# Reloading the residual in single steps, and preferring copies out of PSUM over weight casts

## The chip, the cores and the metric

The kernel runs on one core of a Trainium2 chip. The core has a matrix engine (TensorE, PE in the profile; PEld is its loading of the stationary operand), a vector engine (VectorE, DVE), a scalar engine (ScalarE, ACT), a general engine (GpSimd, POOL) and a queue engine (SyncE, SP), each with an instruction queue of its own, and 16 DMA engines between them. Matmuls write to PSUM, from which DVE and ACT copy or compute into SBUF. The metric is the device time of one execution in microseconds, the median of three runs; smaller is better.

## The reference

Two layers of a decoder trunk over 256 tokens of width 2048, all in fp32. Layer 0 mixes two recurrent branches, layer 1 is a matrix memory (mLSTM). What both do around the mixer is what matters here:

```
for i in range(DEPTH):                       # DEPTH = 2
    hn = rmsnorm(h, norm[i])
    y = mixer_i(hn)                          # layer 1: q, k, v, two gates, mLSTM, head norm, gates
    h = h + y @ w_out[i]                     # output projection, residual add
    pl = rmsnorm(p[i] @ ple_w[i], ple_norm[i])        # p[i]: 256 x 256
    h = h + sigmoid(h @ ple_gate_w[i]) * pl  # gated per-layer embedding
return rmsnorm(h, final_norm)
```

## The kernel before

Every fp32 product is made of three matmuls on parts: each operand x is split into hi, x rounded to the matrix engine's fp32r format, and lo = x - hi, and hi*hi, hi*lo and lo*hi are added up. Weights come in as tiles of 128 x 1024 (`raw`, 512 KB, five buffers, loaded by SP). For each, ACT makes `whi` (line 135) and DVE makes `wlo` (line 136), with four buffers of each. The tokens' operand is split in the same way beforehand (`ahl`, lines 149 and 150). A projection is computed in chunks of 512 output columns; a chunk has two halves of 128 tokens and four quarters of the contraction, and one quarter takes two weight tiles and 24 matmuls (`quarter_tok`, lines 185 to 200). There are three PSUM buffers `mm` and three `mx`.

The program is traced from Python in one order and then planned: a planner lists each engine's instructions in the order in which they would be ready by its own reckoning of times, and the lower number wins among those that are ready. An instruction's number is its place in the trace, less an offset where it stands in `tc.high_priority(offset=...)`. The weight casts of lines 135 and 136 have 400. On the chip each engine then takes its instructions strictly in the planned order, and semaphores hold it where data or a buffer is not there yet. `tc.issue_after(x)` puts an instruction behind x on the same engine.

Side work is written as generators in named lanes. `start` adds one, `step` advances a lane to its next `yield`, `drain` runs it to its end, and `pump`, called once in each quarter, advances every lane by one step, behind the latest cast, matmul and hop of each engine (lines 64 to 85). A transposition from tokens to features is such side work: DVE transposes 32 x 32 blocks into `w` (line 613 or 484), POOL issues a DMA to DRAM (line 600) and four more back into `r` (line 603, a hop), and ACT and DVE finish it (line 631, then 149 and 150; in `to_features` lines 500 and 502).

Layer 1 ends like this, in trace order:

- the last gate projection in the loop of lines 1318 to 1331. Its products `A`, `E`, `B` are in the three `mm` buffers, and partial sums `p1`, `p15` and `g` are in two tiles of the pool tag "h"; lines 274 to 280 form the sums, lines 1323 to 1329 apply the gates, and lane `fm0` to `fm3` transposes each result `u` for the output projection;
- the reload of the residual, lines 1332 to 1336: the hidden state h, which was put into DRAM after layer 0 (`away`), comes back in four tiles `hq` of 128 x 2 x 512 (512 KB each) in the tag "h", whose four buffers until then hold the partial sums and the combined operands of the gate projections;
- the embedding product p[1] @ ple_w[1], `embed`, line 1345: four weight tiles, four groups of 12 matmuls (line 438), one per chunk of 512 columns, each with two token halves in two `mm` buffers. The first half is copied into `pl` by ACT (line 450) and the second by DVE (line 448). The copies have no priority in layer 1 (`first` is None) and 600 in layer 0;
- the output projection, `out_proj`, line 1371, with 16 quarters. Its chunks come from `chunks`: the first two are interleaved, so that chunk 0 is complete after the seventh quarter. Each complete chunk is added to `hq` (line 521), then its transposition starts. The lane "emb", started just before, holds the embedding's norm and gains, and loads rows of gains (line 468).

The reload before:

```
hq = []
for c in range(4):
    t = hp.tile([P, 2, 512], F32, name="hq", tag="h")
    gp.dma_start(out=t, in_=away[c])
    hq.append(t)
```

Of the kernel before, what the change touches and what calls it, by code (L numbers as in the profile page):

```python
# [11 lines left out]
F32 = mybir.dt.float32  # L12
# [7 lines left out]
P = 128  # L20
# [23 lines left out]
def trunk(ctx: ExitStack, tc: tile.TileContext, a, out):  # L44
    nc = tc.nc
    v, s, gp, te, sy = nc.vector, nc.scalar, nc.gpsimd, nc.tensor, nc.sync
# [4 lines left out]
    hp = ctx.enter_context(tc.tile_pool(name="hp", bufs=4))  # L51
# [12 lines left out]
    def start(lane, gen):  # L64
        lanes.setdefault(lane, []).append(gen)

    def step(lane):
        q = lanes.get(lane)
        while q:
            if next(q[0], lanes) is not lanes:  # L70
                return True
            q.pop(0)
        return False
# [8 lines left out]
    def drain(*which):  # L82
        for lane in which:
            while step(lane):
                pass
# [38 lines left out]
    def load_weights(src, pieces=(1, 1), halves=(0, 1), rooms=None):  # L124
        parts = []
        for hf in halves:
            raw = wp.tile([P, 1024], F32, name="raw", tag="raw", bufs=5)
            hi, lo = rooms(hf) if rooms else (wp.tile([P, 1024], F32R, name=n, tag=n) for n in ("whi", "wlo"))
            n = 1024 // pieces[hf]
            for c in range(0, 1024, n):  # L130
                r, h, l = (x[:, c:c + n] for x in (raw, hi, lo))
                sy.dma_start(out=r, in_=block(src, hf * 1024 + c, n))
                with ExitStack() as order:
                    order.enter_context(tc.high_priority(offset=400))
                    last["act"] = s.copy(h, r).ins  # L135
                    last["dve"] = v.tensor_tensor(out=l, in0=r, in1=h.bitcast(F32), op=ALU.subtract).ins  # L136
            parts.append((hi, lo))
        return parts
# [19 lines left out]
    def tokens(x, k, hf):  # L158
        return x[:, k, hf * P:(hf + 1) * P]
# [230 lines left out]
    def load_head(src):  # L390
        praw = tp.tile([P, 512], F32, name="praw", tag="hn", bufs=3)
        raw = wp.tile([P, 1024], F32, name="raw", tag="raw", bufs=5)
        hi, lo = (wp.tile([P, 1024], F32R, name=n, tag=n) for n in ("whi", "wlo"))
        ph, pl, both = act_pair()

        def piece(x, n):
            return x[:, n * T:(n + 1) * T]

        for q, dst, of, n in ((sy, praw, a["pT"][0], 0), (s, raw, src, 0), (gp, raw, src, 1), (s, raw, src, 2),
                              (sy, praw, a["pT"][0], 1), (sy, raw, src, 3)):  # L400
            q.dma_start(out=piece(dst, n), in_=block(of, n * T, T))
        with tc.high_priority(offset=900):
            for n in range(4):
                if n < 2:
                    v.tensor_copy(ph[:, n], piece(praw, n))
                    v.tensor_tensor(out=pl[:, n], in0=piece(praw, n), in1=ph[:, n].bitcast(F32), op=ALU.subtract)
                s.copy(piece(hi, n), piece(raw, n))
                v.tensor_tensor(out=piece(lo, n), in0=piece(raw, n), in1=piece(hi, n).bitcast(F32), op=ALU.subtract)
        return (hi, lo), (ph, pl, both)

    def embed(w, pact, tile_of, first=None):

        pls = []
        for b in range(2):
            head = first and b == 0
            if head:
                part, pact = load_head(w[0])
                parts = [part] + load_weights(w[0], (1, 2), (1,))
            else:
                parts = load_weights(w[b], *(((2, 1),) if first else ()))  # L420
            if first and b:
                first()
            for c, (hi, lo) in enumerate(parts):
                terms = [(hf, k, x, y, 0, 512) for hf in range(2) for k in range(2) for x, y in ((0, 0), (0, 1), (1, 0))]
                if head:
                    terms.sort(key=(lambda t: (t[3], t[3] and t[0], t[1])) if c == 0 else
                               (lambda t: (t[1], t[3] if t[1] == 0 else t[0], t[3])))
                    if c == 0:
                        terms[0:4] = [(hf, 0, x, 0, o, T) for o in (0, T) for x in range(2) for hf in range(2)]
                pool, name = (px, "mx") if first and c == 0 else (pm, "mm")  # L430
                ps = [pool.tile([P, 512], F32, name=name, tag=name) for _ in range(2)]
                halves = []
                for n, (hf, k, x, y, o, w_) in enumerate(terms):
                    mine = [m for m, t in enumerate(terms) if t[0] == hf]
                    with ExitStack() as behind:
                        if first and "pe" in last:
                            behind.enter_context(tc.issue_after(last["pe"]))
                        last["pe"] = te.matmul(ps[hf][:, o:o + w_], tokens(pact[x], k, hf),  # L438
                                               (hi, lo)[y][:, k * 512 + o:k * 512 + o + w_],
                                               start=(n == mine[0]), stop=(n == mine[-1])).ins  # L440
                    if n < mine[-1]:
                        continue
                    pl = tile_of()
                    with ExitStack() as order:
                        if first:
                            order.enter_context(tc.high_priority(offset=600))
                        if hf and (b or not first):
                            v.tensor_copy(pl, ps[hf])
                        else:
                            s.copy(pl, ps[hf])  # L450
                    halves.append(pl)
                pls.append(halves)
        return pls
# [61 lines left out]
    def out_proj(hq, parts, lane):  # L515

        act = {}
        for c, ps in enumerate(parts):
            with tc.high_priority(offset=100):
                for hf in range(2):  # L520
                    v.tensor_tensor(out=hq[c][:, hf], in0=ps[hf], in1=hq[c][:, hf], op=ALU.add)
            start(f"{lane}{c}", to_features(hq[c], c, act, None, lane))
            step(f"{lane}{c}")
        return act
# [17 lines left out]
    def small(n, name, rows=P):  # L542
# [6 lines left out]
    m0_scope = ExitStack()  # L549
    m0 = m0_scope.enter_context(tc.tile_pool(name="m0", bufs=2))  # L550
    pls = embed(a["pw"], None, lambda: p0.tile([P, 512], F32, name="pl", tag="pl"),
                lambda: sy.dma_start(out=prm, in_=a["prm"]))
    identr = cp.tile([P, 8], F32R, name="identr")
# [466 lines left out]
    hq = []  # L1020
# [19 lines left out]

    pe0 = []
    act = out_proj(hq, mixed(), "fe")
    drain("pg")
    e0 = pe0[0]
# [22 lines left out]
    away = []  # L1067
# [25 lines left out]
    with tc.tile_pool(name="m1", bufs=2) as m1:  # L1093
# [32 lines left out]
        for j, ps in enumerate(chunks(a["oqk"], 4, acth, ready(acth, "fg"))):  # L1126
            if j == 0:
                drain("norm")
            t = m1.tile([P, 2, 512], F32, name="tqk", tag="vt", bufs=6)
# [188 lines left out]
        for jj in (0, 2):  # L1318
            us = [m1.tile([P, 2, 512], F32, name="u", tag="vt", bufs=6) for _ in range(2)]
            for b, hf, src in pair(a["oz"], jj):  # L1320
# [4 lines left out]
                for i in range(2):  # L1325
                    c = hf * 8 + 2 * j + i
# [3 lines left out]
                if hf:  # L1330
                    start(f"fm{j}", feature_major(u, "cn", 4 * j, y, 5))
        hq = []
        for c in range(4):
            t = hp.tile([P, 2, 512], F32, name="hq", tag="h")
            gp.dma_start(out=t, in_=away[c])
            hq.append(t)

        pairs = []

        def pl_half():  # L1340
            n = len(pairs)
            pairs.append(pairs[n - 2] if n % 4 > 1 else m1.tile([P, 1024], F32, name="pl", tag="qk", bufs=4))
            return pairs[n][:, n % 4 // 2 * 512:(n % 4 // 2 + 1) * 512]

        pls = embed(a["pw1"], pact, pl_half)
        pss = m1.tile([P, 4, 2], F32, name="pss", bufs=1)

# [21 lines left out]
        step("fm3")  # L1369
        start("emb", embed_norm())  # L1370
        act = out_proj(hq, chunks(a["oo"], 4, y, ready(y, "fm")), "fo")
        drain("emb")

# [59 lines left out]
        y, yh, t, r = (tp.tile([P, 1], F32, name=n, tag=n, bufs=2) for n in ("fy", "fyh", "ft", "fr"))  # L1433
# [22 lines left out]
        yh, t, r = (tp.tile([P, 1], F32, name=n, tag=n, bufs=2) for n in ("fyh", "ft", "fr"))  # L1456
# [131 lines left out]
```

## Time and profile before

| | us |
|---|---|
| median of three runs | 1036.03 |
| lowest and highest of the three | 1033.94, 1036.8 |
| the profiled execution | 1034.75 |
| its span (first to last instruction) | 1033.0 |
| mean granted TensorE clock | 0.996 of full speed |
| last gate projection ends, embedding product starts (line 438) | 833.62 |
| output projection starts (line 196) | 849.67 |
| first sum with the reloaded residual (line 521) | 885.40 |
| issues of the four reloads on POOL (line 1335) | 808.24, 818.35, 835.59, 839.58 |
| reads from HBM over the whole span | 218.11 MB |

The profile is one execution, recorded by the hardware. Times in its views are counted from the span's start. A timeline row is: start, duration, engine, line, operation, written tile <- read tiles, shapes, count, and in brackets the idle time before it on its engine and what ended it. Matmuls overlap, so that the duration of one (0.39 us) is longer than the step from one to the next. In the rows of windows each engine's busy time stands with its number of instructions in brackets. A wait with several causes is put down to the one that came last.

### The profile page before, as it was taken

To read this page: it belongs to the slowest core of one execution; us is meant where nothing else is said; L and a number is where in the kernel's file an instruction comes from. 1 tells how busy PE (TensorE), PEld (TensorE's weight loads), DVE (VectorE), ACT (ScalarE), POOL (GpSimd) and SP (SyncE) were. 2 spreads that over 40 slices of the span, in tenths; PEclk is the share of its full clock that TensorE was granted. 3 is DMA by queue.
4 is the path that set the end of the run, shared out by engine and by line. 5 is a ranking of instruction groups with operands and counts; after the bars stand their busy time and mean duration, and the time that the engine had idled before them with its cause. 6 is when DMAs were issued, how large, how long until landed. Compare 5 with 4: busy or idle time off the path is not lost.

```text
span 1033.0 us, 14470 instructions
## 1 busy us (share of the span) xinstructions
PE 1020.5 (99%) x5206; PEld 847.1 (82%) x5206; DVE 786.8 (76%) x1194; ACT 615.8 (60%) x883; POOL 95.0 (9%) x178
## 2 busy tenths in 40 slices
PE   9999999999999999999999999999999989999996
PEld 8888888888888888887888888888888878888886
DVE  7858968969685776767569987887788886766684
ACT  7675545586964444565557876765565576344562
POOL 0111101011111111111021000000001111111000
PEclk9999999999999999999999999999999999999999
DMA  9987756567788897798797755464666787788652
GB/s 361 332 246 229 222 164 204 187 197 241 225 255 294 274 267 249 235 293 269 231 292 230 220 178 168 154 202 160 210 205 229 238 286 264 215 290 272 200 185 82
DMA packets 68808, 239.00 MB, mean 231 GB/s; under 512 B 8928, under 2 KB 10336, under 8 KB 68736
## 3 DMA queue, kind: packets, MB, share of 16 engines
q1 hardware_dynamic: 55584, 196.51, 58.4%
q0 software_dynamic: 12720, 41.04, 13.2%
q8 instruction: 41, 0.67, 0.3%
q10 hardware_dynamic: 432, 0.52, 0.1%
q14 instruction: 31, 0.25, 0.1%
HBM read 218.11 MB, written 19.92 MB: 230 GB/s over the span
## 4 chain that ended last, share of the span: by engine, by line
PE 93%; DMA 2%; issue 2%; ACT 1%; POOL 1%; DVE 0%; ACTq 0%; POOLq 0%
PE mm L196 21%; PE mm L197 21%; PE mm L198 21%; PE mm L217 9%; PE mx L196 4%; PE mx L197 4%; PE mx L198 4%; PE mx L217 3%; DMA r<-ducn 1%; PE mm L438 1%; PE nu L1241 1%; PE mm L1414 1%; PE mm L1413 1%; PE mm L1412 1%; DMA ducn<-w 1%
## 5 line engine op out<-in xcount | busy, mean ns | idle before, releaser
L136 DVE TENSOR_TENSOR wlo<-raw,whi 128x1024 fp32r<-128x1024 f32 (+1 forms) x341 | 411.8, 1215 | 168.3 <-ACT whi L135 158.6
L135 ACT CAST whi<-raw 128x1024 fp32r<-128x1024 f32 (+1 forms) x341 | 356.0, 1048 | 279.8 <-PE mm L198 184.0
L196 PE MATMUL mm<-whi,ahl 128*128 128x512 f32 x960 | 375.1, 391 | 0.0
L197 PE MATMUL mm<-wlo,ahl 128*128 128x512 f32 x960 | 373.9, 389 | 0.0
L198 PE MATMUL mm<-whi,ahl 128*128 128x512 f32 x960 | 373.6, 389 | 0.0
L196 PEld LDWEIGHTS mm<-whi,ahl 128*128 128x128 f32 x960 | 180.2, 188 | 38.2 <-issue 0.8
L198 PEld LDWEIGHTS mm<-whi,ahl 128*128 128x128 f32 x960 | 180.2, 188 | 37.7
L197 PEld LDWEIGHTS mm<-wlo,ahl 128*128 128x128 f32 x960 | 180.2, 188 | 37.0 <-DVE wlo L136 0.5
L217 PE MATMUL mm<-whi,ahl 128*128 128x512 f32 x320 | 101.2, 389 | 0.0
L217 PEld LDWEIGHTS mm<-whi,ahl 128*128 128x128 f32 x320 | 60.1, 188 | 12.4
L196 PE MATMUL mx<-whi,ahl 128*128 128x512 f32 x160 | 62.2, 389 | 0.0
L197 PE MATMUL mx<-wlo,ahl 128*128 128x512 f32 x160 | 62.2, 389 | 0.0
L198 PE MATMUL mx<-whi,ahl 128*128 128x512 f32 x160 | 62.2, 389 | 0.0
L217 PE MATMUL mm<-wlo,ahl 128*128 128x512 f32 x160 | 62.2, 389 | 0.0
L217 PE MATMUL mx<-whi,ahl 128*128 128x512 f32 x112 | 37.2, 390 | 0.0
L217 PEld LDWEIGHTS mm<-wlo,ahl 128*128 128x128 f32 x160 | 30.0, 188 | 6.3
L198 PEld LDWEIGHTS mx<-whi,ahl 128*128 128x128 f32 x160 | 30.0, 188 | 6.3
L196 PEld LDWEIGHTS mx<-whi,ahl 128*128 128x128 f32 x160 | 30.0, 188 | 6.2
L197 PEld LDWEIGHTS mx<-wlo,ahl 128*128 128x128 f32 x160 | 30.0, 188 | 6.2
L207 DVE TENSOR_TENSOR wlo<-ch,whi 128x1024 fp32r<-128x1024 f32 x20 | 24.1, 1222 | 9.6 <-ACT whi L206 8.9
L206 ACT CAST whi<-ch 128x1024 fp32r<-128x1024 f32 x20 | 21.0, 1051 | 13.1 <-PE mm L217 12.1
L217 PEld LDWEIGHTS mx<-whi,ahl 128*128 128x128 f32 x112 | 21.0, 188 | 4.3
(368 smaller groups left out, 1093.6 us busy)
## 6 DMA issues: line engine op xcount, KB each, us to landing
raw<-in_ew_dram SPq DMA_DIRECT2D x64, 512.0 KB, 5.0
raw<-in_g_dram SPq DMA_DIRECT2D x64, 512.0 KB, 4.9
raw<-in_eo_dram SPq DMA_DIRECT2D x32, 512.0 KB, 5.8
raw<-in_oqk_dram SPq DMA_DIRECT2D x32, 512.0 KB, 4.9
raw<-in_ov_dram SPq DMA_DIRECT2D x32, 512.0 KB, 4.2
raw<-in_oo_dram SPq DMA_DIRECT2D x32, 512.0 KB, 4.9
raw<-in_oog_dram SPq DMA_DIRECT2D x28, 512.0 KB, 4.1
raw<-in_oz_dram SPq DMA_DIRECT2D x28, 512.0 KB, 4.4
```

The lines of the kernel that those rows point to most:

```text
L135: last["act"] = s.copy(h, r).ins
L136: last["dve"] = v.tensor_tensor(out=l, in0=r, in1=h.bitcast(F32), op=ALU.subtract).ins
L196: te.matmul(ps[hf], xh, wh, start=(k == 0), stop=False)
L197: te.matmul(ps[hf], xh, wl, start=False, stop=False)
L198: last["pe"] = te.matmul(ps[hf], xl, wh, start=False, stop=(k == KT - 1)).ins
L206: last["act"] = s.copy(hi, r).ins
L207: last["dve"] = v.tensor_tensor(out=lo, in0=r, in1=hi.bitcast(F32), op=ALU.subtract).ins
L217: last["pe"] = te.matmul(o, x, y, start=(first and k + i == 0), stop=(end and k == n - 1 and i == 2), skip_group_check=True).ins
L438: last["pe"] = te.matmul(ps[hf][:, o:o + w_], tokens(pact[x], k, hf), (hi, lo)[y][:, k * 512 + o:k * 512 + o + w_], start=(n == mine[0]), ...
L1241: te.matmul(ps[:, 0:n], x[:, i, o:o + P], y[:, b, i], start=(b == 0 and x is sh and y is vh), stop=(b == hf and y is vl))
L1412: te.matmul(o, xh, wh, start=(k == 0), stop=False)
L1413: te.matmul(o, xh, wl, start=False, stop=False)
```

## The change

```diff
@@ embed @@
                     with ExitStack() as order:
-                        if first:
-                            order.enter_context(tc.high_priority(offset=600))
+                        order.enter_context(tc.high_priority(offset=600 if first else 450))
                         if hf and (b or not first):
                             v.tensor_copy(pl, ps[hf])
                         else:
@@ out_proj @@
         for c, ps in enumerate(parts):
+            drain("home")
             with tc.high_priority(offset=100):
                 for hf in range(2):
                     v.tensor_tensor(out=hq[c][:, hf], in0=ps[hf], in1=hq[c][:, hf], op=ALU.add)
@@ layer 1, after the last gate projection @@
         hq = []
-        for c in range(4):
-            t = hp.tile([P, 2, 512], F32, name="hq", tag="h")
-            gp.dma_start(out=t, in_=away[c])
-            hq.append(t)
+
+        def home():
+            for _ in range(3):
+                yield
+            for c in range(4):
+                t = hp.tile([P, 2, 512], F32, name="hq", tag="h")
+                gp.dma_start(out=t, in_=away[c])
+                hq.append(t)
+                yield
+
+        start("home", home())
```

The copies of layer 1's embedding out of PSUM get an offset of 450, more than the 400 of the weight casts. The four reloads become a lane "home". The lane starts where the reloads stood, but `embed` does not pump, so it is advanced in the pumps of the output projection: three empty steps, then one reload in each of the fourth to the seventh quarter. By then the sum of chunk 0 is next, and `drain` makes sure that no reload is left. A reload traced in a pump stands behind the latest hop on POOL. Layer 0 has no lane "home", and its copies keep 600, so nothing of it is edited.

## The prediction

> **What bounds the kernel now.** I read the page's first part for the busiest engine, then the list of what TensorE waited for, then the stretch of that wait instruction by instruction.
>
> ```profile
> PE 1020.5 (99%) x5206; PEld 847.1 (82%) x5206; DVE 786.8 (76%) x1194; ACT 615.8 (60%) x883; POOL 95.0 (9%) x178
> ```
> ```profile
> 850.00:1020.00 170.00, 170.00 (x780) 141.88 (x779) 116.96 (x181) 85.27 (x122) 15.92 (x29) 1.00 0.69 220
> 833.60:849.70 16.10, 13.14 (x50) 10.05 (x49) 12.44 (x18) 11.05 (x17) 1.12 (x2) 0.89 0.87 284
> ```
> ```profile
> PE mm L438 <- ACT pl L450: 1.8, 1, 1.8
> PE mm L438 <- DVE pr L280: 1.2, 1, 1.2
> ```
>
> TensorE is busy for 99% of the span. In the windows (columns: length, then busy time and count of PE, weight loads, DVE, ACT, POOL, then granted clock, DMA share, GB/s) it runs without a gap from 850 to 1020 us, so whatever is saved ahead of 850 reaches the end in full. The stretch 833.6 to 849.7 is different: 3 us idle, and a mean granted clock of 0.89. It is the second layer's embedding product (line 438). The two largest waits of TensorE in the whole trace are here: one for an ACT copy out of PSUM (line 450), one for a DVE subtraction (line 280). The timeline of PE shows their places.
>
> ```profile
> 833.62 0.39 PE L438 MATMUL mm<-whi,ahl 128*128 128x512 f32 x1
> ...
> 836.12 0.39 PE L438 MATMUL mm<-whi,ahl 128*128 128x512 f32 x1
> 837.70 0.47 PE L438 MATMUL mm<-whi,ahl 128*128 128x512 f32 x1 [1.19 <-DVE pr L280]
> ...
> 840.31 0.39 PE L438 MATMUL mm<-whi,ahl 128*128 128x512 f32 x1
> 842.46 0.50 PE L438 MATMUL mm<-whi,ahl 128*128 128x512 f32 x1 [1.76 <-ACT pl L450]
> ...
> 849.67 0.39 PE L196 MATMUL mm<-whi,ahl 128*128 128x512 f32 x1
> ```
>
> The product is 48 matmuls in four groups of 12. The first group starts at 833.62 and its twelfth at 836.12: 2.50 us over 11 steps, 0.227 us a matmul, so 48 would take 10.90 us. They take 849.67 - 833.62 = 16.05, that is 5.15 us too long: a first stall of 837.70 - 836.35 = 1.35 (836.35 is 836.12 plus one step), 0.12 in the second group, a second stall of 842.46 - 840.54 = 1.92, and 1.76 in the last 24 matmuls, which take 7.21 instead of 5.45. The last part is the clock:
>
> ```profile
> 843.00:843.50 0.50, 0.50 (x3) 0.38 (x2) 0.50 (x2) 0.50 (x2) 0.00 (x0) 1.00 1.03 410
> 843.50:844.00 0.50, 0.50 (x3) 0.39 (x2) 0.50 (x2) 0.50 (x1) 0.00 (x0) 0.58 1.02 410
> 844.00:845.00 1.00, 1.00 (x4) 0.81 (x3) 1.00 (x2) 1.00 (x3) 0.00 (x0) 0.50 1.04 410
> ```
>
> A microsecond after the second stall the granted clock drops to 0.50, and it had been 1.00 after the first. Why was the copy of line 450 late? The timelines of ACT and DVE (in brackets: idle time before, and its releaser):
>
> ```profile
> 837.58 0.72 ACT L1323 ACTIVATE u<-pr,rth 128x512 f32<-128x512 f32 x1 [0.65 <-DVE pr L280]
> 840.09 0.51 ACT L631 ACTIVATE xr<-r,prm 128x256 f32<-128x256 f32 x1 [1.78 <-DMA r<-ducn]
> 840.50 1.03 ACT L135 CAST whi<-raw 128x1024 fp32r<-128x1024 f32 x1
> 841.44 0.50 ACT L631 ACTIVATE xr<-r,prm 128x256 f32<-128x256 f32 x1
> 841.85 0.56 ACT L450 COPY pl<-mm 128x512 f32<-128x512 f32 x1
> ```
> ```profile
> 835.73 1.22 DVE L136 TENSOR_TENSOR wlo<-raw,whi 128x1024 fp32r<-128x1024 f32 x1
> 836.87 0.68 DVE L280 TENSOR_TENSOR pr<-mm,pr 128x512 f32<-128x512 f32 x1
> ...
> 843.10 1.28 DVE L448 COPY pl<-mm 128x512 f32<-128x512 f32 x2
> ```
>
> Two things come together. The products need PSUM buffers, of which there are three. The second half of the first group was complete near 836.5, but DVE's copy of it (line 448) ran only at 843.10, behind a cast remainder and the mixer's arithmetic. So the third group had to take the buffer of the second group's first half, and ACT's copy of that stood behind line 631 (which waited 1.78 us for the transposed features to land), a weight cast of 1.03 and a second line 631.
>
> **The change, part by part.**
>
> *Copies preferred.* The four ACT and four DVE copies of the embedding go from no priority to 450, ahead of the weight casts' 400. No instruction is added or lengthened. DVE's copy of the first group then goes next behind line 280's subtraction, which ends at 837.55: at about 837.5 instead of 843.10, so a buffer is free near 838.2, ahead of the 840.54 at which TensorE asks for it. The second stall goes: 1.92 us. What is late next is the ACT copy of the second group's first half, ready near 839.4: even behind line 631 at 840.09 it would end near 841.1, and the half after next needs its buffer only at 840.54 + 6 x 0.227 = 841.9. The drop of the clock behind it goes with it, I take it: 1.76. What hides the casts that step back is slack: the first output-projection matmul would need its cast at 849.67 - 3.68 = 845.99, and each copy put ahead costs a cast 0.57 on ACT or 0.68 on DVE. That cover is thin on DVE: its 12.44 us of the stretch would stand in 16.10 - 3.68 = 12.42. Part of it can go later (the two transposes of line 613 and the last copy), so I bound the remaining stall between 0 and the 1.22 of one cast remainder and take 0, since DVE now idles in this stretch while TensorE has to wait. If the cover is gone, TensorE waits those 1.22.
>
> *First stall.* It waits for line 280 behind a cast remainder (835.73) in DVE's order. Line 280 already has priority 450 and the change does not touch it, so I keep the 1.35 us. Bounds: 0 and -1.35 less.
>
> *Reload moved.* Four DMA issues leave their place ahead of the embedding and go into the pumps of the output projection, behind the last transposing hop on POOL.
>
> ```profile
> 831.13 2.21 POOL L603 DMA_DIRECT2D r<-ducn  x4 [6.95 <-ACT whi L135]
> 835.59 0.56 POOL L1335 DMA_DIRECT2D hq<-dh  x1 [2.24 <-DVE u L1324]
> 839.58 0.56 POOL L1335 DMA_DIRECT2D hq<-dh  x1 [3.43 <-DVE u L1324]
> 850.33 0.54 POOL L600 DMA_DIRECT2D ducn<-w  x1 [10.20 <-DVE w L613]
> 854.58 2.21 POOL L603 DMA_DIRECT2D r<-ducn  x4 [3.71 <-DMA ducn<-w]
> 856.78 1.10 POOL L468 DMA_DIRECT2D row<-in_rows_dram  x2
> 891.87 0.54 POOL L600 DMA_DIRECT2D dfo<-w  x1 [33.99 <-DVE w L484]
> ```
> ```profile
> 885.40 0.69 DVE L521 TENSOR_TENSOR hq<-mm,hq 128x512 f32<-128x512 f32 x1
> ```
> ```profile
> raw<-in_oo_dram SPq DMA_DIRECT2D x32, 512.0 KB, 4.9
> hq<-dh POOLq DMA_DIRECT2D x4, 512.0 KB, 6.9
> ```
> ```profile
> 829.17 87.29 SPq L132 DMA_DIRECT2D raw<-in_oo_dram  x32
> ```
> ```profile
> 850.00:860.00 10.00, 10.00 (x46) 8.29 (x45) 5.40 (x7) 6.34 (x12) 3.84 (x7) 1.00 0.85 259
> 860.00:870.00 10.00, 10.00 (x46) 8.29 (x45) 7.69 (x9) 7.71 (x16) 0.00 (x0) 1.00 0.88 319
> ```
>
> On POOL the four issues cost 4 x 0.56 = 2.24 us, and POOL is idle for 33.99 us ahead of 891.87: free. At the old place they held nothing that mattered, as the hop behind them waited for its transposed tile until 850.33. What their going gives is DMA room: the hop of line 600 that ran beside them took 6.95 us until the next issue, the one at 850.33 only 3.71. The data that line 631 waits for may come between 0 and 3.24 us sooner; I count nothing for it, because the copies no longer stand behind line 631, and as insurance it only makes the second stall's end surer. At the new place they are issued in a row behind 857.9 (856.78 + 1.10), the last by 860.1, and land 6.9 later at 867; if they follow the pumps instead, the first goes near 865 and lands near 872. The first sum that reads them runs at 885.40, or 881.7 after the gain: 10 us spare at least. No instruction but that sum waits for them; on DVE the sum would hold the casts behind it. Each reload writes a buffer that is free by then, so no new wait stands on POOL either.
>
> The DMA engines pay: 4 x 512 KB is 2.1 MB, at the 410 GB/s of the full rows above 5.1 us of all engines. From 850 to 870 they have 1.5 + 1.2 = 2.7 us free, so the weights could run up to 2.4 us late near 870. The weights' lead covers it: the output projection's first load is issued at 829.17 and its first cast is at 840.50, 11.3 us later, against 4.9 from issue to landing: 6.4 us spare. Cost taken: 0; bounds 0 and 5.1. A page of the Trainium skill speaks against the move: "DMA: Bandwidth & Descriptors", section "Queues, rings and completion order", says that an engine takes turns between the queues that have work, a packet at a time. By that rule a weight load beside the reload would take about 9.8 us instead of 4.9 (an estimate), still inside 11.3, and the sum stays; no row of this case shows the turns themselves.
>
> *Sum.* 1.92 + 1.76 = 3.68 us: span 1033.0 to 1029.3, the profiled execution 1034.75 (1.75 outside the span) to 1031.1. The median of the three runs is 1036.03, 1.28 above the profiled one, and from it 1032.3.
>
> **The rivals.**
>
> *The first stall goes too* (the planner, with copies in other places, puts line 280 ahead of the remainder at 835.73): all 5.15 us, 1030.9. For it: DVE could have started line 280 1.14 us sooner. Against: nothing in the change lifts it.
>
> *The clock drop stays.* If the stall of 1.92 is not what lowers the clock, or the first stall's 1.35 is enough, only 1.92 is gained: 1034.1. For it: the first stall stays. Against: the clock was 1.00 after it for 5 us. The Trainium skill, "TensorE: Matmul & The Clock Gate", section "Part 1: The HAM clock gate", puts the drop after an idle window of about 3.4 us; by that rule a stall of 1.92 would not cause it and this rival would hold, but the trace, with 0.50 a microsecond after 1.92, does not agree.
>
> *The change does not do what it says:* the copies still end up behind line 631, and it waits as long: 0 gained, 1036.0. For it: preference decides only between instructions that are ready in the planner's reckoning, and the real wait for the DMA isn't in it. Against: DVE's copy depends on no DMA.
>
> *Slower: weights starved by the reload.* Its place is 857 to 875 us. If a weight load takes over 11.3 us from issue to landing, TensorE waits; the whole 5.1 us of reload traffic then stands in its path, with a clock drop of 1.76 behind it: 5.1 + 1.76 - 3.68 = 3.2 more, 1039.2. For it: the engines are 85 to 88% busy there. Against: the 6.4 us of lead, and the 2.4 us of backlog.
>
> **How the numbers follow.** Forecast 1032.3: 0.52. First stall too: 0.13. Clock drop stays: 0.12. No effect: 0.12. Slower: 0.11. The range goes from 1030.3, a little under the second case, to 1036.1, just over no effect; it takes in the 1.22 of a late remainder and leaves out the slower case. About 0.3%, 3.1 us, is what a measurement of this kernel can tell from no change: faster by more means under 1032.9. The forecast lies close to that line, so I give it 0.7 of its 0.52, with the second case nearly whole and a little of the third: 0.50. Slower: 0.10. The rest, 0.40, is within.
>
> **What would show it.** Right: line 448's first copy right behind line 280 near 837.5; no wait of PE for line 450; the step from the second to the third group 0.23 us; a granted clock of 1.00 from 838 to 850; the first line 196 near 846; the reloads on POOL behind the rows; the first sum near 882. Wrong: line 280's wait gone (second case); 0.50 in the clock after a short stall (third); line 450 still behind line 631 (fourth); PE waiting for a cast between 860 and 885 (slower). A late cast at the first matmuls of line 196 would mean that DVE has become the bound of this stretch.

## The result and the profile after

The changed kernel takes 1030.97 us, the median of 22 runs (1029.79 to 1040.09), against 1034.77 for the kernel before in 22 runs beside it (1033.13 to 1038.55). The ratio is 0.997, with a 95% interval of 0.9956 to 0.9983: 3.8 us between the medians, and about 3 by the ratio. The forecast was 0.9964 of the time before. The size is right; the profiles show that the way to it was another.

The profiled execution of the changed kernel is one of the few long ones: 1036.66 us, with a span of 1034.9. Sixteen of the 22 runs are under 1032. So it shows what can still go wrong. A second profile of the same kernel (label both_again, 1029.85, span 1028.1) shows a run in which it doesn't; that run is among the shortest, some 1.1 us under the median. Two transposing hops matter in what follows: the first is issued on POOL at 808.79 in the profile of before, the second at 823.63 (line 600). First the waits of TensorE and its timeline in the first profile, from the start of the embedding product to the start of the output projection:

```profile
PE mm L438 <- ACT pl L449: 2.9, 1, 2.9
```
```profile
835.85 0.39 PE L438 MATMUL mm<-whi,ahl 128*128 128x512 f32 x1
...
842.45 0.39 PE L438 MATMUL mm<-whi,ahl 128*128 128x512 f32 x1
845.75 0.50 PE L438 MATMUL mm<-whi,ahl 128*128 128x512 f32 x1 [2.92 <-ACT pl L449]
...
851.59 0.39 PE L196 MATMUL mm<-whi,ahl 128*128 128x512 f32 x1
```

The first stall, for line 280, is gone. The second is not: it has moved on by six matmuls, to the second half of the third group, and is longer, 3.07 us (845.75 less 842.45 and one step of 0.23). The product takes 15.74 us instead of the bare 10.90. The timeline of ACT in the same profile says why (line 449 is the copy that was line 450):

```profile
838.91 1.04 ACT L135 CAST whi<-raw 128x1024 fp32r<-128x1024 f32 x1
844.33 0.91 ACT L631 ACTIVATE xr<-r,prm 128x256 f32<-128x256 f32 x2 [4.38 <-DMA r<-ducn]
845.14 0.56 ACT L449 COPY pl<-mm 128x512 f32<-128x512 f32 x1
```

The copy still stands behind line 631 in ACT's queue, and line 631 waits 4.38 us for the hop to land. In the second profile the same hop, the second one, lands in time. Its waits of TensorE, all of them, and the same places:

```profile
PE st L97 <- PEq L1586: 0.8, 1, 0.8
PE mx L438 <- ACT whi L407: 0.3, 1, 0.3
```
```profile
833.69 0.39 PE L438 MATMUL mm<-whi,ahl 128*128 128x512 f32 x1
...
844.61 0.50 PE L196 MATMUL mm<-whi,ahl 128*128 128x512 f32 x1
```
```profile
838.85 0.91 ACT L631 ACTIVATE xr<-r,prm 128x256 f32<-128x256 f32 x2 [1.14 <-DMA r<-ducn]
839.66 0.57 ACT L449 COPY pl<-mm 128x512 f32<-128x512 f32 x1
```

From 833.69 to 844.61 is 10.92 us: no loss at all, although ACT's queue is in the same order. What differs is the landing, 5.2 us after the start of the product here (838.85 - 833.69) and 8.5 in the first profile (844.33 - 835.85). The two waits that are left lie in the first microseconds. Against the profile of before the product ends 5.06 us sooner (844.61 against 849.67) and the span is 4.9 us shorter, nearly the whole 5.15 us of the product's loss.

Most of the late landing can be followed back. The rows of the two hops in the first profile, then in the second:

```profile
825.27 1.31 ACT L631 ACTIVATE xr<-r,prm 128x256 f32<-128x256 f32 x3 [2.82 <-DMA r<-ducn]
827.13 0.69 DVE L150 TENSOR_TENSOR ahl<-xr,ahl 128x512 fp32r<-128x512 f32 x1 [2.31 <-ACT ahl L149]
829.22 0.70 DVE L613 STREAM_TRANSPOSE w<-u 128x512 f32<-128x512 f32 x1
830.22 0.56 POOL L600 DMA_DIRECT2D ducn<-w  x1 [10.91 <-DVE w L613]
```
```profile
820.20 1.30 ACT L631 ACTIVATE xr<-r,prm 128x256 f32<-128x256 f32 x3
824.31 0.71 DVE L613 STREAM_TRANSPOSE w<-u 128x512 f32<-128x512 f32 x1
825.31 0.56 POOL L600 DMA_DIRECT2D ducn<-w  x1 [9.45 <-DVE w L613]
```

In the changed kernel the second hop's last transposition (line 613) stands on DVE behind the finish of the first hop (line 150). In the first profile the first hop lands late, line 631 waits 2.82 us for it, and so the second hop is issued 5.6 us before the product's start (835.85 - 830.22) instead of 8.4 (833.69 - 825.31). That is 2.75 of the 3.3 us by which it lands later. In the kernel before both transpositions, at 821.12 and 822.62, are ahead of line 150 at 829.06: the reload's move has also changed the planned order of DVE.

The reload at its new place costs nothing that can be seen. POOL issues it behind the rows, as forecast, and the DMA engines are full for a while, in the first profile:

```profile
859.14 1.11 POOL L467 DMA_DIRECT2D row<-in_rows_dram  x2
860.24 1.05 POOL L1339 DMA_DIRECT2D hq<-dh  x2
...
```
```profile
870.00:880.00 10.00, 10.00 (x46) 8.29 (x45) 8.45 (x11) 7.00 (x12) 0.00 (x0) 1.00 1.02 408
```

In the window from 870 to 880 the DMA share is 1.02, and TensorE is busy for all of the 10 us.

### The profile page after: what moved, and what is told of

It reads as the page before. It is cut to its first block, busy times and chain, and to the rows that moved or that the text cites. A ratio compares the mean times of both kernels' runs of the same rounds, so it can differ in the third digit from the quotient of the medians.

```text
span 1034.9 us, 14474 instructions
## 1 busy us (share of the span) xinstructions
PE 1022.1 (99%) x5206; PEld 849.1 (82%) x5206; DVE 786.1 (76%) x1194; ACT 615.8 (59%) x883; POOL 94.8 (9%) x178
## 4 chain that ended last, share of the span: by engine, by line
PE 96%; DMA 2%; issue 1%; ACT 1%; POOL 0%; ACTq 0%; DVE 0%; POOLq 0%
PE mm L196 21%; PE mm L198 21%; PE mm L197 21%; PE mm L217 11%; PE mx L217 4%; PE mx L198 4%; PE mx L196 4%; PE mx L197 4%; PE mm L438 1%; PE nu L1241 1%; PE mm L1421 1%; PE mm L1420 1%; PE mm L1419 1%; PE mx L438 1%; DMA ducn<-w 1%
```

## The experiments

**Two theories.** H: the hop decides. What stalls the embedding product are ACT's and DVE's queues, held by a transposed tile that has not landed; the reload's traffic makes it land late. C: the copies decide, as the prediction had it. Kernels were made to tell them apart; line numbers shift by a few between kernels.

**The copies' priority alone** (copies_only):

```diff
-                        if first:
-                            order.enter_context(tc.high_priority(offset=600))
+                        order.enter_context(tc.high_priority(offset=600 if first else 450))
```

> The kernel before with the copies' priority alone; the reload stays ahead of the embedding product. In the planned order only DVE's copies (line 447 here) move forward, ACT's four copies keep their places behind line 630. Theory H (the hop decides: what stalls the embedding product is ACT's copy behind the transposed features' landing, and the reload's traffic makes that landing late): the priority only moves the stall from the third group's first half to its second, about 1.4 us later, so 1 to 2 us gained at most: 1032.8 to 1034.8. Rival C (the copies decide, as in the prediction): second stall and clock drop gone, 3.7 us gained: 1031.1, and nothing is left for the reload.

Measured: 1034.28 (12 runs, 1032.19 to 1035.8) against 1035.84 before; ratio 0.9986, 0.9974 to 0.9998. Its waits of TensorE, and its ACT timeline:

```profile
PE mm L438 <- DVE pr L280: 1.6, 1, 1.6
PE mm L438 <- ACT pl L449: 1.0, 1, 1.0
```
```profile
842.20 0.51 ACT L630 ACTIVATE xr<-r,prm 128x256 f32<-128x256 f32 x1 [2.33 <-DMA r<-ducn]
842.61 1.03 ACT L135 CAST whi<-raw 128x1024 fp32r<-128x1024 f32 x1
843.55 0.50 ACT L630 ACTIVATE xr<-r,prm 128x256 f32<-128x256 f32 x1
843.96 0.56 ACT L449 COPY pl<-mm 128x512 f32<-128x512 f32 x1
```

ACT's order is that of before to the last instruction: line 631 (630 here), cast, 631, copy. Priority only chooses among what is ready in the planner's reckoning, so there the copy's data must have come later than the hop's (the planner's times themselves are not on record). On DVE the first copy moved ahead, and so TensorE asks for ACT's copy six matmuls later: 1.0 us of wait instead of 1.8, and both stalls are still there. H's size holds, C falls.

**The moved reload alone** (reload_only): the changed kernel with the first edit undone.

```diff
-                        order.enter_context(tc.high_priority(offset=600 if first else 450))
+                        if first:
+                            order.enter_context(tc.high_priority(offset=600))
```

> The kernel before with the moved reload alone; the copies keep no priority. Theory H: line 280's stall (1.35 us) goes, because the first hop lands about 2 us sooner without the reload beside it and ACT's casts are no longer late; the wait for ACT's copy stays and may grow, because DVE's transposition for the next hop now stands behind the first hop's landing: between 1032 and 1036, with runs far apart. Rival C: nothing but DMA room, the same as before within 1 us: 1034.8.

Measured: 1034.13, but with runs from 1029.73 to 1040.4; ratio 0.9998, 0.9976 to 1.0019. Its waits, and DVE's line 280 for the first of the two sums:

```profile
PE mm L438 <- ACT pl L450: 2.2, 1, 2.2
PE mx L438 <- ACT whi L407: 0.9, 1, 0.9
```
```profile
831.96 0.69 DVE L280 TENSOR_TENSOR pr<-mm,pr 128x512 f32<-128x512 f32 x1 [0.41 <-PE mm L217]
```

The stall for line 280 is gone without any edit to DVE's priorities: here DVE waits for TensorE, not the other way. In the kernel before the same instruction ran at 833.12, right behind a cast remainder; the remainders were late because ACT's casts had stood behind line 631 of the first hop. The rows of before, from ACT's and from DVE's timeline:

```profile
825.08 0.51 ACT L631 ACTIVATE xr<-r,prm 128x256 f32<-128x256 f32 x1 [4.85 <-DMA r<-ducn]
825.49 1.03 ACT L135 CAST whi<-raw 128x1024 fp32r<-128x1024 f32 x1
```
```profile
831.99 1.22 DVE L136 TENSOR_TENSOR wlo<-raw,whi 128x1024 fp32r<-128x1024 f32 x1
833.12 0.68 DVE L280 TENSOR_TENSOR pr<-mm,pr 128x512 f32<-128x512 f32 x1
```

In reload_only ACT finds the first hop landed, and the first cast behind it runs 2.8 us sooner (822.70 against 825.49):

```profile
821.00 1.30 ACT L632 ACTIVATE xr<-r,prm 128x256 f32<-128x256 f32 x3
822.70 1.05 ACT L135 CAST whi<-raw 128x1024 fp32r<-128x1024 f32 x1
```

The move also changed ACT's planned order, but that doesn't explain the gain: three of line 631 (632 here) now stand ahead of this cast, where before it was one. What is gone is the wait of 4.85 us. The stall for ACT's copy stays, and the runs scatter over 10 us with it. Over the runs the gain of the one is lost in the other.

**The changed kernel again** (both_again), for the second profile shown above.

> The changed kernel once more, for a second profile of it. Theory H: a median near 1031; where the profile falls in a run near 1030.5, line 631 waits under 2 us for the hop and TensorE under 1 us for the copy, with the clock at 1.00 throughout; where it falls near 1037, TensorE waits 2 to 3 us as in the first profile. Rival C: the spread is not tied to this place, and a run near 1030.5 shows the same wait of 2.9 us for the copy.

Measured: 1031.18 (12 runs, 1029.66 to 1040.25); ratio 0.9966, 0.9947 to 0.9985. The profile has no wait of TensorE in the product, as H wanted of a short run. Of the 34 runs of this kernel so far, 25 are under 1032, four from 1032 to 1034 and five from 1036.6 to 1040.3.

**The copies ahead of the hop's finish in ACT's queue** (copies_ahead): the changed kernel, and the features' finish is issued behind the last embedding copy on ACT. As `put` joins `last`, behind whose entries `pump` puts the side work, the other side work of the output projection follows that copy on ACT too.

```diff
+                            put = s.copy(pl, ps[hf]).ins
+                            if not first:
+                                last["put"] = put
...
         r = yield from landed((u[:, 0], u[:, 1]), f"du{gain}{first}", lag)
+        with ExitStack() as behind:
+            if "put" in last:
+                behind.enter_context(tc.issue_after(last["put"]))
```

> The changed kernel, and the features' finish on ACT (line 636 here, 631 in the changed kernel) is put behind the last of ACT's embedding copies in ACT's queue, so that no copy can stand behind a landing DMA. Theory H: TensorE waits for nothing in the embedding product, whatever the hop does; no run near 1037; a median of 1030.0 to 1030.8, and a spread of 1.5 us. Rival C: the same as the changed kernel, median and spread.

Measured: 1029.6 (5 runs, 1029.43 to 1029.85); ratio 0.9942, 0.9928 to 0.9955. ACT in this kernel:

```profile
837.91 0.59 ACT L449 COPY pl<-mm 128x512 f32<-128x512 f32 x1 [0.26 <-PE mm L438]
...
840.63 0.59 ACT L449 COPY pl<-mm 128x512 f32<-128x512 f32 x1 [0.26 <-PE mm L438]
...
843.35 0.59 ACT L449 COPY pl<-mm 128x512 f32<-128x512 f32 x1 [0.26 <-PE mm L438]
843.83 1.31 ACT L636 ACTIVATE xr<-r,prm 128x256 f32<-128x256 f32 x3
```

Every copy now waits for TensorE alone, 0.26 us, and line 636 (631) follows behind the last without a wait. The median is a little under what H expected, and the tail is gone, as H wanted. Beside the last two kernels below (copies_ahead_2) it measured 1029.94 (6 runs, 1029.54 to 1031.26; ratio 0.9941, 0.9924 to 0.9957); no run of the 11 reaches 1032. The median is as expected there; the spread, 1.7 us, is smaller than that of the two kernels below (2.4 and 1.9), where the expectation had it no smaller.

> The changed kernel with ACT's order (copies_ahead) once more, beside the two kernels above. Theory H: the first hop still stands in ACT's queue here, so some runs may lose up to 1 us to it: a median of 1029.5 to 1030.3 and a spread no smaller than the two above.

**The same order, one edit of the change at a time.** With ACT in order, what are the two edits still worth? order_only adds it to the kernel before, copies_and_order to copies_only, reload_and_order to reload_only.

> The kernel before with one edit that the change does not have: the features' finish on ACT (line 636 here) stands behind the last of ACT's embedding copies. Reload in its old place, copies without priority. Theory H: the second stall (1.9 us) and the clock's drop (1.8) go, line 280's stall (1.2 to 1.6) stays, because it comes from the first hop's late landing; DVE's late copies cost up to 1 us: 1031.0 to 1032.6. Rival R (the reload's DMA traffic must leave as well, the order alone does not help): 1034 or more.

> The same order on ACT and the copies' priority, with the reload in its old place. Theory H: only line 280's stall is left: 1031.0 to 1031.6, and against the changed kernel with the order (1029.6) the difference of 1.4 to 2 us is what moving the reload is worth. Rival R: 1033 or more.

> The same order on ACT and the moved reload, without the copies' priority. Theory H: DVE's first copy comes behind the mixer's arithmetic but before TensorE asks for its buffer, or up to 0.6 us after: 1029.6 to 1030.3, so that the priority is worth under 0.6 us once ACT is in order. Rival P (the priority on DVE is what frees the buffers): 1031.5 or more, with a wait of PE for line 448.

| kernel | median us, runs | range | ratio to before, 95% interval |
|---|---|---|---|
| order_only | 1034.96, 12 | 1032.3 to 1036.91 | 0.9986, 0.997 to 1.0003 |
| copies_and_order | 1032.97, 12 | 1031.95 to 1036.74 | 0.9974, 0.9959 to 0.9988 |
| reload_and_order | 1030.6, 10 | 1029.95 to 1032.62 | 0.9956, 0.9941 to 0.9971 |

The third came out a little above what H wanted. Its profile has 0.2 us of wait for line 448, so rival P falls; what the priority is still worth beside the order, 0.9956 against the 0.9942 of copies_ahead in another batch, these runs can't tell from nothing. The first two missed by 2.4 and 1.4 us above H's upper ends: order_only lies where rival R had it (1034 or more), and copies_and_order just short of that (1033). While the first hop is late, the order alone helps little. The waits of order_only show where the rest is:

```profile
PE mm L438 <- DVE pr L280: 1.6, 1, 1.6
PE mx L438 <- ACT whi L407: 1.3, 1, 1.3
PE mm L217 <- ACT whi L135: 1.0, 1, 1.0
PE st L97 <- PEq L1584: 0.8, 1, 0.8
PE mm L217 <- DVE wlo L136: 0.8, 1, 0.8
PE mm L438 <- DVE pl L448: 0.2, 1, 0.2
```

No wait for ACT's copy is left. What is left comes from the first hop: ACT waits for it until 828.62 (825.08 in before), and the weight casts behind it reach TensorE late, 1.0 and 0.8 us inside the last gate projection (line 217), ahead of line 280's 1.6. The expectation had counted only the last of the three. The hop's write to DRAM (line 600) lands slower where the reload runs beside it; the DMA issues from 800 to 850 us (KB each, median us to landing) of before, order_only and both_again:

```profile
ducn<-w POOLq DMA_DIRECT2D x2, 512.0 KB, 6.9
```
```profile
ducn<-w POOLq DMA_DIRECT2D x2, 512.0 KB, 8.3
```
```profile
ducn<-w POOLq DMA_DIRECT2D x3, 512.0 KB, 4.5
```

Over all profiles this median is 6.7 to 8.3 us in the five kernels with the reload in the old place and 4.5 to 6.1 in the seven profiles with it in the new.

**The first hop's finish out of the way as well.** If the reload's place matters only through the held queues, it must stop mattering when the first hop's finish also stands late in the queues. both_late_old_place is copies_and_order, both_late_new_place is copies_ahead, each with

```diff
-                    start(f"fm{j}", feature_major(u, "cn", 4 * j, y, 5))
+                    start(f"fm{j}", feature_major(u, "cn", 4 * j, y, 7 if j == 1 else 5))
```

> Reload in its old place, copies' priority, ACT's order as in copies_and_order, and the finish of the first hop (lane fm1) steps two pumps later, so that ACT and DVE take it behind the last weight casts of the gate projection. Theory H: the moved reload is worth something only because the first hop's landing holds ACT's and DVE's queues; with both finishes out of the way the reload's place is worth nothing: 1029.4 to 1030.2, no waits of TensorE from 815 on, and the same as the next kernel within 0.5 us. Rival M (the reload's DMA traffic or its issues on POOL cost something by themselves): 1031.5 or more, as in copies_and_order (1033.0).

> The same with the reload in its new place. Both theories: 1029.4 to 1030.0.

Measured, beside each other: 1031.27 (6 runs, 1029.45 to 1031.85; ratio 0.9948, 0.9933 to 0.9964) in the old place and 1030.11 (6 runs, 1029.9 to 1031.82; 0.9943, 0.9927 to 0.9958) in the new. The old place is 1.1 us above H's range and just under rival M's 1031.5, and the medians lie 1.2 us apart where H had 0.5; the new place is 0.1 above its range. The intervals of the two lie over each other. In favour of H are the traces and the gain: neither kernel has a wait of TensorE from 800 to 850, and the old place has 0.9948 against the 0.9974 of copies_and_order, which differs from it in the first hop's finish alone (another batch, and the intervals overlap a little). In the old place the first hop still lands late, and it now holds only itself:

```profile
823.79 1.06 ACT L135 CAST whi<-raw 128x1024 fp32r<-128x1024 f32 x1 [0.30 <-PE mm L217]
826.18 1.31 ACT L635 ACTIVATE xr<-r,prm 128x256 f32<-128x256 f32 x3 [1.34 <-DMA r<-ducn]
```

The casts ahead of it are through at 824.85. So a kernel with the reload where it was is 5.1 us faster than before (1036.4 beside it). Whether the new place is worth up to 1.2 us more, the difference of the medians, six runs each cannot tell.

## Why the prediction was right, and where it was not

The time moved by the forecast amount, but three terms behind the sum were wrong, and they made up for each other.

- **"Copies preferred": wrong.** The step that failed is that the copies would go ahead of the casts and free the buffers in time. On DVE they did, though a cast remainder still stands between line 280 and the first copy (in copies_only at 839.02, between 838.42 and 840.15). On ACT not one instruction changed places (copies_only against before), since the planner had the hop's data landed before the copy's. "Even behind line 631 at 840.09 it would end near 841.1" put the copy straight behind the first line 631, where a cast and a second 631 still stood between, and took the landing of one execution for fixed. This was the third rival's mechanism, though its 0 was too low: the priority alone gives 0.14%, 1.4 us.
- **"First stall: I keep the 1.35": wrong.** It goes with the reload (reload_only). The step overlooked was upstream: line 280 was late because cast remainders were, those because ACT's casts were, and those because line 631 of the first hop waited 4.85 us at 825. The chain of waits of before, followed back past 830, names the hop, line 631 and ACT's casts as its links.
- **"Reload moved: I count nothing for it": wrong.** The two edits are worth 1.4 us and nothing alone (0.9986 and 0.9998) and 3.5 together (0.9966). The move takes away the first stall, the priority lets TensorE ask for ACT's copy six matmuls later, and only with both does the copy mostly come in time. The bound of 0 to 3.24 us held for the second hop's way from its issue to line 631: 16.5 us before (840.09 - 823.63), 13.5 to 14.8 in the three profiles of after, both_again and reload_only. But there the hop is also issued later, behind the first hop's finish, so that, counted from the product's start, its data comes 1.3 us sooner than before in the second profile, 0.1 sooner in reload_only and 2.0 later in the first profile. With ACT in order the reload's move is worth some 3 us more (0.9974 with the reload in the old place, 0.9942 in the new).
- **The clock's drop goes with the stall: right.** The second profile has no stall and no drop, the first has 3.07 us of stall and then 1.75 us of loss in the last 18 matmuls (851.59 - 845.75 = 5.84 against 4.09).
- **Weights starved by the reload: rightly set aside.** TensorE was fed at a DMA share of 1.02.
- **The reload's new place: held.** The first sum that reads it starts at 880.51 in the second profile, where the prediction had it near 882. (Its spare "10 us at least" is 9.7 by its own numbers, 881.7 - 872.)
- **DVE's thin cover: held.** In the second profile, without a late hop, the product loses nothing.

So the product of the second profile is the second case of the prediction, all 5.15 us gained, and that of the first profile is the case in which the change does not reach the copies. The median gains 3.8 us, in between; where a median run loses its 1.1 us against the second profile, no trace here shows. That the forecast median agrees is therefore luck in good part. The second hop's late landing in the first profile comes mostly from the first hop. Why the first hop itself lands late there is open: its write is issued at the same time before the product, 25.1 us, in both profiles, with the same traffic planned, and no run varied it alone. The first profile's product ends 7.0 us after the second's (851.59 against 844.61): 4.8 of them are lost in the product, and 2.2 before it, as it begins later (835.85 against 833.69); these go back to the start of the program (last section).

## What to carry to other kernels

An engine with an ordered queue waits where its next instruction waits: before giving priority to a copy, look at what stands ahead of it in the final order, and above all for an instruction that waits for a DMA, since a planner that reckons the landing early can put it there. Such an instruction belongs behind everything urgent that is ready about the same time; here one ordering edge, added to the change, gave 1029.6 to 1029.9 with no run over 1031.3, where the change without it gave 1031 with a tail to 1040. It has to cover every such wait: in the kernel before the same edge gave almost nothing (0.9986), as an earlier hop still held the queues. And when a stall waits for a busy engine, follow that engine's own lateness upstream before calling the stall untouched.

## What the runs showed of the hardware

The granted clock fell to 0.50 for some 3 us after stalls of TensorE of 1.92 (before), 2.38 (reload_only) and 3.07 us (the changed kernel's first profile), and stayed at 1.00 after 1.78 us (order_only) and 1.74 (copies_only). Each is counted like the 1.92 in the prediction, from one step behind the last matmul's start to the next start: in reload_only 842.30 - 839.69 - 0.23, in order_only 841.24 - 839.23 - 0.23. The windows of reload_only and of order_only, just behind their stalls:

```profile
842.00:844.00 2.00, 1.70 (x4) 1.41 (x5) 0.26 (x1) 2.00 (x4) 0.00 (x0) 0.59 0.70 279
844.00:846.00 2.00, 2.00 (x6) 1.55 (x6) 1.59 (x2) 0.88 (x3) 0.00 (x0) 0.56 0.03 6
```
```profile
842.00:844.00 2.00, 2.00 (x10) 1.68 (x9) 2.00 (x5) 1.37 (x2) 0.56 (x1) 1.00 1.02 406
```

The rule of the Trainium skill that the prediction weighed, "TensorE: Matmul & The Clock Gate", "Part 1: The HAM clock gate", asks for an idle window of about 3.4 us. Here stalls of 1.92 and 2.38 us were enough, so that the one of 1.92 cost nearly twice its length (1.92 + 1.76). Five profiles don't make a threshold: 1.78 and 1.92 lie close together, and before had another stall of 1.35 us five microseconds earlier.

The start of the program also differs from run to run. The first group of 12 matmuls in the chain took 4.36 us in the first profile of the changed kernel and 2.73 in the second, and ended 2.2 us later, at 10.42 instead of 8.25 (chain of waits, in order of time):

```profile
6.06 4.36 PE mx L438 x12
```
```profile
5.52 2.73 PE mx L438 x12
```
